# The first norm of a hybrid decoder block, rebuilt with two projections side by side and every engine in program order

## The chip, the cores and the metric

The kernel runs on one core of one Trainium2 chip. The metric is the device time of one launch in microseconds (us); the median of several runs is compared. PE (with PEld, its weight loads) is TensorE, DVE is VectorE, ACT is ScalarE, POOL is GpSimd and SP is SyncE, which issues the loads spoken of here.

## The reference

One decoder block over 512 tokens of width 1024, in float32. Only its beginning matters here:

```python
def rms_norm(x, g):
    y = xf * lax.rsqrt(jnp.mean(xf * xf, axis=-1, keepdims=True) + RMS_EPS)
    return y * g

h = rms_norm(x, ln1_g)
p = h @ w_in                  # 20 column tiles of 128 in the kernel
y_rwkv = rwkv7_mixer(p[..., :RWKV_COLS], ...)      # 14 of them
y_attn = rms_norm(swa_sink_attention(p[..., RWKV_COLS:] + b_attn, sinks), attn_norm_g)
x = x + concat(y_rwkv, y_attn) @ w_out
x = x + peer_ffn(rms_norm(x, ln2_g), ...)          # product-key retrieval, 16384 experts
return rms_norm(x, lnf_g)
```

The mixer needs a decay from a small projection (column tile 0, the low-rank inputs), and for each pair of heads j the tiles r, k and v (2+3j, 2+3j+1, 2+3j+2). Tile 3 is the first k. Inside the mixer a triangular 64x64 matrix is inverted for each chunk of 64 tokens; this inverse uses small masks.

## The kernel before, in words

x arrives transposed, as eight pieces `xT[:, k, :]` of 128 features x 512 tokens (256 KB each). The weight of the norm goes onto each piece (`h`, line 269 of the profile's numbering), the factor 1/rms of each token does not: it is put on after the projection, as `rb`, so that projections can run before the norm's sum is known. Products run in a split form: each float32 operand becomes a high part, cast on ScalarE (`split`, L166), and a low part, a subtraction on VectorE (L167), and each product is three (L176 to L178): high with high, low with high, high with low. A weight tile of one projection is two halves of 256 KB (`load_w`, L243) in three buffers `w`, with four buffers each for high and low parts.

The norm (`rms`) squares each piece on ScalarE (`take`, L216 and L219) into one of three buffers `n1sq` and adds the squares up on an engine given by name, here VectorE (L220); the last addition is always VectorE's. `scale` sums over the partitions with one-column products (`n1ss`, L225) and takes the reciprocal root in some eleven small VectorE instructions (`rsqrt`, L198 to L206). `spread` broadcasts the result with products (`n1b`, L232), and ScalarE copies it to `rb` (L283).

Projection 0 is written out, with the order of TensorE's instructions as traced (`manual_schedule` with TensorE alone), followed by `scale` and `spread`. For all else in the front the framework's list scheduler chooses the order on each engine: by priority in order of tracing, filling idle time with what is ready. `lora` then takes projection 0 through `shifted` (times `rb`, L307; the token shift, L308 and L309), tanh into `lw`, a memset of `lw` on GpSimd (L326) and the decay products (L330). `prepare(0)` follows with projections 3, 2 and 4. PSUM has two buffers with the tag `proj`; one is given back when `shifted` has multiplied it by `rb`.

The masks of the inverse, `lmask` and `id32`, are made on GpSimd at the very beginning: 20 memsets (L142), 20 selections (L144), 20 further selections (L147) and four for `id32` (L134). Their first reader is the inverse in `products(0)` (L473).

Loads are issued by SyncE in this order: the vectors, pieces 0 and 1 of x, the two halves of weight tile 0, pieces 2 to 7, the sinks, then what the front needs next.

Behind the front come a second block with TensorE's order written out (the output projection and the second norm, from about 312 us) and two with all engines in program order (retrieval and the expert sums).

Of the kernel before, what the change touches and what calls it, by code (L numbers as in the profile page):

```python
# [7 lines left out]
F32 = mybir.dt.float32  # L8
F32R = mybir.dt.float32r
# [8 lines left out]
S = 512  # L18
# [57 lines left out]
def _emit(ctx, tc, A, out, dbg, stop):  # L76
# [18 lines left out]
    for k in range(2):  # L95
        SY.dma_start(xT[:, k, :], A["xT"][:, k, :])
    sink = consts.tile([128, 8], F32, name="sink")

    def vcol(c):
        return vec[:, c:c + 1]  # L100
# [27 lines left out]


    lmask = consts.tile([128, 5, 32], F32, name="lmask")  # L130
    id32 = consts.tile([128, 32], F32, name="id32")
    for q in range(4):
        rows = slice(32 * q, 32 * q + 32)
        GP.affine_select(out=id32[rows], in_=ones[rows, :32], pattern=[[1, 32]],  # L134
                         compare_op=OP.is_equal, fill=0.0, base=0, channel_multiplier=-1)
    for lv in range(5):
        b = 1 << lv
        n = 32 // (2 * b)
        for q in range(4):
            rows = slice(32 * q, 32 * q + 32)  # L140
            m = lmask[rows, lv, :].rearrange("p (n w) -> p n w", w=2 * b)
            GP.memset(lmask[rows, lv, :], 0.0)  # L142

            GP.affine_select(out=m[:, :, b:2 * b], in_=ones[rows, :n * b].rearrange("p (n w) -> p n w", w=b),  # L144
                             pattern=[[-2 * b, n], [0, b]], compare_op=OP.is_ge, fill=0.0,
                             base=0, channel_multiplier=1)
            GP.affine_select(out=m[:, :, b:2 * b], in_=m[:, :, b:2 * b],  # L147
                             pattern=[[2 * b, n], [0, b]], compare_op=OP.is_ge, fill=0.0,
                             base=b - 1, channel_multiplier=-1)
# [87 lines left out]

    def load_w(src, name="w"):
        his, los = [], []
        for hf in range(2):  # L240
            ks = slice(4 * hf, 4 * hf + 4)
            w = wst.tile([128, 4, 128], F32, name=name, tag="w", bufs=3)
            SY.dma_start(w, src[:, ks])  # L243
            whi = wst.tile([128, 4, 128], F32R, name=name + "h", tag="wh", bufs=4)
            wlo = wst.tile([128, 4, 128], F32R, name=name + "l", tag="wl", bufs=4)
            split(whi, wlo, w)
            his += [whi[:, k] for k in range(4)]
            los += [wlo[:, k] for k in range(4)]
        return his, los

    first = {}

    def proj(i, m=128):
        whi, wlo = first.pop(i) if i in first else load_w(A["w_in"][i])
        p = pt("proj", "pj")
        yield from mm3_(p[:m], whi, wlo, hhi, hlo, m=m)
        return p[:m]


    first[0] = load_w(A["w_in"][0])  # L260
    for k in range(2, KD):
        SY.dma_start(xT[:, k, :], A["xT"][:, k, :])
    SY.dma_start(sink, A["sink"])

    take, scale, spread = rms(xp, KD, D, "n1", V)
    hhi, hlo = hl("h")
    for k in range(KD):
        h = xp.tile([128, S], F32, name="h", tag="h", bufs=3)
        V.tensor_scalar(h, xT[:, k, :], vcol(C_LN1 + k), None, op0=OP.mult)
        split(hhi[:, k, :], hlo[:, k, :], h)  # L270
        take(k, xT[:, k, :])
    with tc.manual_schedule(engines={mybir.EngineType.PE}):
        p0 = proj(0)
        while True:
            try:
                next(p0)
            except StopIteration as e:
                p0 = e.value
                break
        scale()  # L280
        pb = spread()
# [39 lines left out]

    def lora():
        yield from shifted(0, la, prep, p=p0)
# [1164 lines left out]
```

## Time and profile before

| | |
|---|---|
| median of 3 runs | 1629.78 us (1628.6 to 1633.54) |
| the profiled execution | 1630.73 us, span 1629.0 us |
| TensorE busy | 1572.6 us, 97% |
| VectorE busy | 1286.1 us, 79% |
| GpSimd busy | 742.4 us, 46% |
| ScalarE busy | 652.5 us, 40% |
| granted TensorE clock, mean | 0.995 |

The profile is of one execution. Its own time and its span differ by what lies around the first and the last instruction. Ends of products are modelled, so two neighbours overlap in the rows; the pitch from start to start is what one of them costs.

### The profile page before, as it was taken

How to read it: one execution, taken by the hardware profiler on the slowest of the kernel's cores; microseconds unless marked ns; L12 is line 12 of the kernel's file. 1: busy time of each engine (PE TensorE's matmuls, PEld its weight loads, DVE VectorE, ACT ScalarE, POOL GpSimd, SP SyncE). 2: the span in 40 equal slices, each digit the busy share in tenths (PEclk: the TensorE clock that was granted, in tenths of full speed). 3: DMA queues.
4: the chain of work that ended last, by engine and by line, in shares of the span. 5: the costliest groups of instructions: out<-in, count | busy, mean ns of one | idle time of the engine just before them, and what ended most of it. 6: DMA issues, size and time to landing. Idle time of an engine off the chain costs nothing.

```text
span 1629.0 us, 30768 instructions
## 1 busy us (share of the span) xinstructions
PE 1572.6 (97%) x11869; PEld 1366.7 (84%) x11869; DVE 1286.1 (79%) x2497; ACT 652.5 (40%) x1092; POOL 742.4 (46%) x711
## 2 busy tenths in 40 slices
PE   7999999899999889999999999999999999999997
PEld 4777777797999888888988888888888888888886
DVE  6666567756899999999677788777878877887896
ACT  5333345544444344454433333333333333333334
POOL 5121123244676512222155555555655556556582
PEclk9999999999999999999999999999999999999999
DMA  4111110333232269999999888889998988989793
GB/s 143 53 42 42 59 48 2 129 124 103 79 104 91 98 214 336 348 323 354 320 345 351 304 309 320 322 299 316 331 308 301 333 312 303 321 303 339 236 311 136
DMA packets 180548, 371.18 MB, mean 228 GB/s; under 512 B 17840, under 2 KB 102320, under 8 KB 180144
## 3 DMA queue, kind: packets, MB, share of 16 engines
q1 hardware_dynamic: 137488, 226.71, 40.6%
q0 software_dynamic: 36864, 134.23, 22.9%
q10 hardware_dynamic: 6048, 8.26, 1.4%
q8 instruction: 93, 1.52, 0.4%
q14 instruction: 55, 0.45, 0.1%
HBM read 333.62 MB, written 35.52 MB: 227 GB/s over the span
## 4 chain that ended last, share of the span: by engine, by line
PE 50%; DVE 11%; DMA 3%; issue 1%; ACT 1%; POOL 1%; SPq 0%; DVEq 0%; ACTq 0%
PE acc L1359 10%; PE acc L1358 10%; PE acc L1357 10%; PE pA L178 7%; PE pA L176 7%; PE pA L177 7%; DVE O L1228 3%; DVE ul L167 2%; DVE scr L1182 2%; DVE P L1233 2%; DMA u<-in_uT_dram 2%; DMA row<-in_vB_dram,ix 1%; DMA v<-in_vB_dram 0%; PE pG L1255 0%; POOL row L1169 0%
## 5 line engine op out<-in xcount | busy, mean ns | idle before, releaser
L178 PE MATMUL pA<-h2hi,ul 128*128 128x384 f32 x1024 | 346.2, 338 | 9.9 <-DVE ul L167 5.6
L176 PE MATMUL pA<-h2hi,uh 128*128 128x384 f32 x1024 | 350.3, 342 | 1.5 <-ACT actd L969 1.5
L177 PE MATMUL pA<-h2lo,uh 128*128 128x384 f32 x1024 | 344.1, 336 | 0.0
L1169 POOL DMA_INDIRECT row<-in_u_dram,ix x128 | 175.2, 1369 | 285.7 <-DVE scr L1182 247.7
L1359 PE MATMUL acc<-vl,wh 128*128 128x512 f32 x768 | 300.3, 391 | 1.5 <-DVE vl L167 1.5
L1358 PE MATMUL acc<-vh,wl 128*128 128x512 f32 x768 | 300.0, 391 | 0.2 <-DVE wl L167 0.2
L1357 PE MATMUL acc<-vh,wh 128*128 128x512 f32 x768 | 298.9, 389 | 1.3 <-ACT vh L166 1.3
L1169 POOL DMA_INDIRECT row<-in_vB_dram,ix x128 | 196.1, 1532 | 141.1 <-DVE x L1180 115.7
L167 DVE TENSOR_TENSOR vl<-v,vh 128x1024 fp32r<-128x1024 f32 x128 | 213.9, 1672 | 35.2 <-ACT vh L166 34.4
L178 PEld LDWEIGHTS pA<-h2hi,ul 128*128 128x128 f32 x1024 | 192.8, 188 | 14.8 <-DVE ul L167 10.5
L176 PEld LDWEIGHTS pA<-h2hi,uh 128*128 128x128 f32 x1024 | 193.0, 188 | 4.7 <-ACT actd L969 1.6
L177 PEld LDWEIGHTS pA<-h2lo,uh 128*128 128x128 f32 x1024 | 193.2, 189 | 3.0
L1180 DVE SCALAR_TENSOR_TENSOR x<-row,ac,x 128x1024 f32<-128x1024 f32 x128 | 173.2, 1353 | 7.9 <-DMA row<-in_vB_dram,ix 6.0
L1359 PEld LDWEIGHTS acc<-vl,wh 128*128 128x128 f32 x768 | 144.1, 188 | 32.2 <-DVE vl L167 2.2
L1357 PEld LDWEIGHTS acc<-vh,wh 128*128 128x128 f32 x768 | 144.2, 188 | 30.0 <-ACT vh L166 1.6
L1358 PEld LDWEIGHTS acc<-vh,wl 128*128 128x128 f32 x768 | 144.1, 188 | 29.4 <-DVE wl L167 0.6
L1182 DVE SCALAR_TENSOR_TENSOR scr<-row,h2g 128x1024 f32<-128x1024 f32 x128 | 158.2, 1236 | 1.3
L166 ACT CAST uh<-u 128x1024 fp32r<-128x1024 f32 x128 | 133.9, 1046 | 62.2 <-PE pA L177 29.5
L167 DVE TENSOR_TENSOR ul<-u,uh 128x1024 fp32r<-128x1024 f32 x109 | 134.0, 1230 | 20.1 <-ACT uh L166 17.0
L166 ACT CAST vh<-v 128x1024 fp32r<-128x1024 f32 x128 | 134.0, 1048 | 0.3 <-DMA gts<-gates 0.3
L969 ACT ACTIVATE act<-pA 128x384 f32<-128x384 f32 x86 | 42.2, 491 | 131.6 <-PE pA L178 131.5
L1256 ACT ACTIVATE gst<-pG 128x512 f32<-128x512 f32 x96 | 55.8, 597 | 97.6 <-PE pG L1255 95.9
(725 smaller groups left out, 2621.0 us busy)
## 6 DMA issues: line engine op xcount, KB each, us to landing
u<-in_uT_dram SPq DMA_DIRECT2D x128, 512.0 KB, 6.4
v<-in_vB_dram SPq DMA_DIRECT2D x128, 512.0 KB, 5.9
gts<-gates SPq DMA_DIRECT2D x384, 64.0 KB, 4.5
gates<-gst SPq DMA_DIRECT2D x11, 2048.0 KB, 11.5
w<-in_w_in_dram SPq DMA_DIRECT2D x40, 256.0 KB, 2.8
wq<-in_wq_dram SPq DMA_DIRECT2D x16, 512.0 KB
acts<-actd ACTq DMA_DIRECT2D x42, 192.0 KB, 6.3
act<-acts SPq DMA_DIRECT2D x42, 192.0 KB, 7.5
```

What stands on the lines that cost most here:

```text
L166: (hi_eng or SC.copy)(dst_hi, src)
L167: (lo_eng or V).tensor_tensor(out=dst_lo, in0=src, in1=dst_hi.bitcast(F32), op=OP.subtract)
L176: mm(ps, whi[k][:, :m], ahi[:, k], start=k == 0, stop=False)
L177: mm(ps, whi[k][:, :m], alo[:, k], start=False, stop=False)
L178: mm(ps, wlo[k][:, :m], ahi[:, k], start=False, stop=k == KD - 1)
L1169: GP.indirect_dma_start(r_, None, A["vB"].rearrange("b p d -> (b p) d") if w_ else A["u"], bass.IndirectOffsetOnAxis(ap=ix[:, w_, jj:jj + ...
L1180: V.scalar_tensor_tensor(x2[:, 0, :], r_, ac[:, jj:jj + 1], x2[:, 0, :], op0=OP.mult, op1=OP.add)
L1182: V.scalar_tensor_tensor(scr, r_, 1.0, h2g, op0=OP.mult, op1=OP.mult, accum_out=ac[:, jj:jj + 1])
L1256: SC.activation(gst[:, :, :, t4 * 4:t4 * 4 + 4].rearrange("p n g t -> p (n g) t"), p.rearrange("p t e -> p e t"), AF.Copy, scale=1.0 / GS)
L1357: mm(o, wh[:, ts], vh[:, ds_], start=b == 0, stop=False)
L1358: mm(o, wl[:, ts], vh[:, ds_], start=False, stop=False)
L1359: mm(o, wh[:, ts], vl[:, ds_], start=False, stop=b == 127)
```

## The change

The masks move from the beginning into `lora`, traced behind the first `shifted` and ahead of `lw`. The loads of x and of the weight tiles 0 and 3 are interleaved in one list. The loop over that list is traced with all five engines in program order, and the norm's additions go to GpSimd, but for the last. The products of projection 3 are traced beside those of projection 0, three pieces behind, and all of them ahead of the norm's sums. `prepare(0)` takes projection 3 as given. `load_w` is cut into `load_half` and `split_half`, which do together what it did.

```diff
-    for k in range(2):
-        SY.dma_start(xT[:, k, :], A["xT"][:, k, :])
...
-    lmask = consts.tile([128, 5, 32], F32, name="lmask")
-    id32 = consts.tile([128, 32], F32, name="id32")
-    for q in range(4):
...
+    def load_half(src, hf, name="w"):
+        w = wst.tile([128, 4, 128], F32, name=name, tag="w", bufs=3)
+        SY.dma_start(w, src[:, 4 * hf:4 * hf + 4])
+        return w
+
+    def split_half(w, name="w"):
+        whi = wst.tile([128, 4, 128], F32R, name=name + "h", tag="wh", bufs=4)
+        wlo = wst.tile([128, 4, 128], F32R, name=name + "l", tag="wl", bufs=4)
+        split(whi, wlo, w)
+        return [whi[:, k] for k in range(4)], [wlo[:, k] for k in range(4)]
...
-    first[0] = load_w(A["w_in"][0])
-    for k in range(2, KD):
-        SY.dma_start(xT[:, k, :], A["xT"][:, k, :])
+    ns = ExitStack()
+    ns.enter_context(tc.manual_schedule(engines={mybir.EngineType.Pool, mybir.EngineType.DVE, mybir.EngineType.Activation,
+                                                 mybir.EngineType.PE, mybir.EngineType.SP}))
+    wt = {}
+    arrive = (0, (0, 0), 1, (0, 1), 2, (3, 0), 3, 4, 5, (3, 1), 6, 7)
+    for a in arrive:
+        if isinstance(a, int):
+            SY.dma_start(xT[:, a, :], A["xT"][:, a, :])
+        else:
+            wt[a] = load_half(A["w_in"][a[0]], a[1])
     SY.dma_start(sink, A["sink"])
 
-    take, scale, spread = rms(xp, KD, D, "n1", V)
+    take, scale, spread = rms(xp, KD, D, "n1", GP)
     hhi, hlo = hl("h")
-    for k in range(KD):
-        h = xp.tile([128, S], F32, name="h", tag="h", bufs=3)
-        V.tensor_scalar(h, xT[:, k, :], vcol(C_LN1 + k), None, op0=OP.mult)
-        split(hhi[:, k, :], hlo[:, k, :], h)
-        take(k, xT[:, k, :])
-    with tc.manual_schedule(engines={mybir.EngineType.PE}):
-        p0 = proj(0)
...
+    early = {0: ([], []), 3: ([], [])}
+    for a in arrive:
+        if isinstance(a, int):
+            h = xp.tile([128, S], F32, name="h", tag="h", bufs=3)
+            V.tensor_scalar(h, xT[:, a, :], vcol(C_LN1 + a), None, op0=OP.mult)
+            split(hhi[:, a, :], hlo[:, a, :], h)
+            take(a, xT[:, a, :])
+        else:
+            for x, y in zip(early[a[0]], split_half(wt.pop(a))):
+                x += y
+    p03 = {i: pt("proj", "pj") for i in (0, 3)}
+    two = {i: mm3_(p03[i], *early[i], hhi, hlo) for i in (0, 3)}
+    for n in range(KD + 3):
+        next(two[0], None)
+        if n >= 3:
+            next(two[3], None)
+    scale()
+    pb = spread()
+    ns.close()
...
     def lora():
-        yield from shifted(0, la, prep, p=p0)
+        yield from shifted(0, la, prep, p=p03[0])
+
+
+        for q in range(4):
+            rows = slice(32 * q, 32 * q + 32)
+            GP.affine_select(out=id32[rows], in_=ones[rows, :32], pattern=[[1, 32]],
+                             compare_op=OP.is_equal, fill=0.0, base=0, channel_multiplier=-1)
+        for lv in range(5):
...
     def prepare(j):
         k = prep.tile([128, S], F32, name="k", tag="k", bufs=2)
-        yield from shifted(2 + 3 * j + 1, k, prep)
+        yield from shifted(2 + 3 * j + 1, k, prep, p=p03[3] if j == 0 else None)
```

## Rows read from the trace of the kernel before

**Rows 1.** The page's first part: busy time of each engine, its share of the span, and instructions.

```profile
PE 1572.6 (97%) x11869; PEld 1366.7 (84%) x11869; DVE 1286.1 (79%) x2497; ACT 652.5 (40%) x1092; POOL 742.4 (46%) x711
```

**Rows 2.** Busy time by stage. Columns: the stretch in us from the span's start, its length, then busy us (and instructions) of PE, PEld, DVE, ACT and POOL, the granted TensorE clock, the DMA engines' busy share and GB/s.

```profile
28.40:60.00 31.60, 31.60 (x190) 21.84 (x189) 22.82 (x53) 13.12 (x22) 3.46 (x11) 1.00 0.17 56
60.00:300.00 240.00, 235.20 (x4406) 177.07 (x4406) 157.34 (x416) 107.02 (x256) 57.16 (x96) 1.00 0.12 38
300.00:340.00 40.00, 35.07 (x288) 32.75 (x285) 26.03 (x70) 20.23 (x40) 11.38 (x8) 0.96 0.58 211
```

**Rows 3.** TensorE's products in order of time, 0 to 60 us. Columns here and in the other timelines: start us, us, engine, line, operation, out<-in, shapes, count, and in brackets the idle time before and what ended it.

```profile
10.55 0.63 PE L178 MATMUL pj<-hhi,wl 128*128 128x512 f32 x1
10.97 0.63 PE L176 MATMUL pj<-hhi,wh 128*128 128x512 f32 x1
...
17.14 0.67 PE L176 MATMUL pj<-hhi,wh 128*128 128x512 f32 x2
...
21.54 0.95 PE L225 MATMUL n1ss<-ones,n1acc 128*128 128x1 f32 x8
...
22.66 0.40 PE L176 MATMUL pj<-hhi,wh 128*128 128x512 f32 x1
...
24.06 0.39 PE L176 MATMUL pj<-hhi,wh 128*128 128x512 f32 x1
...
28.22 0.39 PE L178 MATMUL pj<-hhi,wl 128*128 128x512 f32 x1
28.45 0.40 PE L176 MATMUL pj<-hhi,wh 128*128 128x512 f32 x1
```

**Rows 4.** VectorE in order of time, 0 to 34 us.

```profile
7.80 1.49 DVE L167 TENSOR_TENSOR wl<-w,wh 128x512 fp32r<-128x512 f32 x2 [2.16 <-ACT wh L166]
...
14.44 0.47 DVE L269 TENSOR_SCALAR h<-xT,vec 128x512 f32<-128x512 f32 x1
...
15.43 0.47 DVE L269 TENSOR_SCALAR h<-xT,vec 128x512 f32<-128x512 f32 x1
15.83 0.68 DVE L167 TENSOR_TENSOR hlo<-h,hhi 128x512 fp32r<-128x512 f32 x1
16.43 0.68 DVE L220 TENSOR_TENSOR n1acc<-n1acc,n1sq 128x512 f32<-128x512 f32 x1
...
20.23 0.68 DVE L167 TENSOR_TENSOR hlo<-h,hhi 128x512 fp32r<-128x512 f32 x1
...
22.52 0.16 DVE L198 TENSOR_SCALAR rsq<-n1ss 128x4 f32<-128x4 f32 x1 [0.41 <-PE n1ss L225]
22.60 0.68 DVE L167 TENSOR_TENSOR wl<-w,wh 128x512 fp32r<-128x512 f32 x1
23.20 0.17 DVE L201 TENSOR_SCALAR rsq<-rsq 128x4 int32<-128x4 int32 x1
...
25.19 0.20 DVE L206 SCALAR_TENSOR_TENSOR n1rs<-rsq 128x4 f32<-128x4 f32 x1
...
27.40 0.69 DVE L307 TENSOR_TENSOR pr<-pj,rb 128x512 f32<-128x512 f32 x1 [0.69 <-ACT rb L283]
```

**Rows 5.** ScalarE in order of time, 0 to 34 us.

```profile
4.12 0.63 ACT L216 ACTIVATE n1acc<-xT 128x512 f32<-128x512 f32 x1 [2.04 <-DMA xT<-in_xT_dram]
7.15 0.62 ACT L166 CAST wh<-w 128x512 fp32r<-128x512 f32 x1 [2.40 <-DMA w<-in_w_in_dram]
...
14.94 0.62 ACT L166 CAST hhi<-h 128x512 fp32r<-128x512 f32 x1 [0.32 <-DVE h L269]
15.59 0.63 ACT L219 ACTIVATE n1sq<-xT 128x512 f32<-128x512 f32 x1
16.13 0.60 ACT L166 CAST hhi<-h 128x512 fp32r<-128x512 f32 x1
```

**Rows 6.** GpSimd's groups by line, 0 to 60 us (line, operation, out<-in, shapes, count | busy us, mean ns | idle before), and, as the last two rows, from its timeline the first selections for a mask and the first instruction on GpSimd that reads one.

```profile
L144 POOL TENSOR_SCALAR_AFFINE_SELECT lmask<-ones 32x16 f32<-32x16 f32 x20 | 8.6, 430 | 1.2
L147 POOL TENSOR_SCALAR_AFFINE_SELECT lmask<-lmask 32x16 f32<-32x16 f32 x20 | 6.3, 316 | 1.2
L142 POOL MEMSET lmask<- 32x32 f32 x20 | 2.8, 140 | 0.9
...
3.49 1.19 POOL L134 TENSOR_SCALAR_AFFINE_SELECT id<-ones 32x32 f32<-32x32 f32 x4
...
60.13 0.74 POOL L473 TENSOR_TENSOR Lb<-LC,lmask 128x256 f32<-128x256 f32 x1
```

**Rows 7.** GpSimd in order of time, 322 to 332 us: its nearest instructions with two tiles as inputs, the first three beside a busy VectorE.

```profile
323.51 3.22 POOL L853 TENSOR_TENSOR n2acc<-n2acc,n2sq 128x256 f32<-128x256 f32 x3 [27.84 <-ACT n2sq L852]
...
330.02 0.76 POOL L853 TENSOR_TENSOR n2acc<-n2acc,n2sq 128x256 f32<-128x256 f32 x1
330.72 2.41 POOL L167 TENSOR_TENSOR wql<-wq,wqh 128x1024 fp32r<-128x1024 f32 x1
```

**Rows 8.** Busy time and granted clock around the kernel's longest early stop of TensorE (columns as in rows 2).

```profile
318.00:322.00 4.00, 0.99 (x9) 0.79 (x7) 0.78 (x2) 0.00 (x0) 0.00 (x0) 1.00 0.95 394
322.00:324.00 2.00, 1.20 (x5) 1.23 (x6) 1.41 (x4) 1.32 (x4) 0.49 (x1) 0.58 1.02 418
324.00:326.00 2.00, 2.00 (x12) 2.00 (x12) 1.27 (x1) 1.96 (x3) 1.82 (x3) 0.57 0.79 322
```

**Rows 9.** The same view for a stretch of the first norm; the last two columns are the DMA engines.

```profile
14.00:22.00 8.00, 6.52 (x24) 3.75 (x23) 8.00 (x15) 5.08 (x9) 6.94 (x19) 1.00 0.04 14
```

More of the change, by code (lines that the diff above doesn't have):

```diff
@@ L127, in _emit @@
     V.tensor_copy(bones[:, 64:128], hind[:, 1:2].to_broadcast([128, 64]))
-    lmask = consts.tile([128, 5, 32], F32, name="lmask")
-    id32 = consts.tile([128, 32], F32, name="id32")
-    for q in range(4):
[L133 to L149, printed above, removed]
     c_ = consts.tile([128, 64], F32, name="c_")
@@ L240, in load_w @@
         for hf in range(2):
[L241 to L248, printed above, removed]
+            h_, l_ = split_half(load_half(src, hf, name), name)
+            his += h_
+            los += l_
         return his, los
-    first = {}
     def proj(i, m=128):
-        whi, wlo = first.pop(i) if i in first else load_w(A["w_in"][i])
+        whi, wlo = load_w(A["w_in"][i])
         p = pt("proj", "pj")
@@ L257, in proj @@
         return p[:m]
-    first[0] = load_w(A["w_in"][0])
-    for k in range(2, KD):
-        SY.dma_start(xT[:, k, :], A["xT"][:, k, :])
+    ns = ExitStack()
[8 more added lines that the diff above has]
+            wt[a] = load_half(A["w_in"][a[0]], a[1])
     SY.dma_start(sink, A["sink"])
-    take, scale, spread = rms(xp, KD, D, "n1", V)
+    take, scale, spread = rms(xp, KD, D, "n1", GP)
     hhi, hlo = hl("h")
-    for k in range(KD):
-        h = xp.tile([128, S], F32, name="h", tag="h", bufs=3)
-        V.tensor_scalar(h, xT[:, k, :], vcol(C_LN1 + k), None, op0=OP.mult)
-        split(hhi[:, k, :], hlo[:, k, :], h)
-        take(k, xT[:, k, :])
-    with tc.manual_schedule(engines={mybir.EngineType.PE}):
-        p0 = proj(0)
[L274 to L281, printed above, removed]
+    early = {0: ([], []), 3: ([], [])}
[17 more added lines that the diff above has]
+    ns.close()
     rb = prep.tile([128, S], F32, name="rb", tag="rb")
@@ L320, in _emit @@
     ld = [prep.tile([128, S], F32, name=f"ld{t}", tag=f"ld{t}") for t in range(NT)]
+    lmask = consts.tile([128, 5, 32], F32, name="lmask")
+    id32 = consts.tile([128, 32], F32, name="id32")
     def lora():
-        yield from shifted(0, la, prep, p=p0)
+        yield from shifted(0, la, prep, p=p03[0])
[4 more added lines that the diff above has]
+        for lv in range(5):
+            b = 1 << lv
+            n = 32 // (2 * b)
+            for q in range(4):
+                rows = slice(32 * q, 32 * q + 32)
+                m = lmask[rows, lv, :].rearrange("p (n w) -> p n w", w=2 * b)
+                GP.memset(lmask[rows, lv, :], 0.0)
+                GP.affine_select(out=m[:, :, b:2 * b], in_=ones[rows, :n * b].rearrange("p (n w) -> p n w", w=b),
+                                 pattern=[[-2 * b, n], [0, b]], compare_op=OP.is_ge, fill=0.0,
+                                 base=0, channel_multiplier=1)
+                GP.affine_select(out=m[:, :, b:2 * b], in_=m[:, :, b:2 * b],
+                                 pattern=[[2 * b, n], [0, b]], compare_op=OP.is_ge, fill=0.0,
+                                 base=b - 1, channel_multiplier=-1)
         lw = prep.tile([128, S], F32, name="lw", tag="t2")
```

## Prediction

> **What bounds the kernel now.** I read the page first, then the busy time by stage, then the order of each engine over the first 31 us. Over the whole span TensorE is busy 97% [rows 1]. By stage the last place with room is the front: from 28.4 us to 300 us TensorE is idle only 4.8 of 271.6 us (31.60 of 31.60 and 235.20 of 240.00 busy), and in the hand-over around 320 us 4.9 of 40 [rows 2]. So a delay or gain that TensorE takes before 28.4 us is passed on: there is no slack behind it that could swallow it, and little idle time that a new order there could win. What is to be read is therefore one number: when TensorE may start its third projection, the one traced for `r`.
>
> In the kernel before this is at 28.45 us [rows 3]. There are two PSUM buffers with the tag `proj`. Projection 0 and projection 3 hold both, and the third needs the one that the multiply by `rb` gives back. That multiply starts at 27.40 and ends at 28.09 [rows 4]. Projection 3's last product starts just ahead of 28.45, so here the chain of the norm and TensorE's work end together: while VectorE computes the reciprocal root (22.52 to 25.39), TensorE is fed by projection 3 [rows 3, 4]. That cover is what the change spends.
>
> **The chain behind the sums.** From the first sum product (21.54) to the end of the multiply (28.09) it is 6.55 us, of which 0.60 is a weight split that lies inside (22.60 to 23.20) [rows 3, 4]. Alone the chain takes 5.95 us. So the third projection starts at (start of the sums) + 5.95, and the break-even is a start of the sums at 28.45 - 5.95 = 22.5 us.
>
> **The change: the loop in program order.** For one piece of x the order is now: VectorE h, ScalarE hi, VectorE lo, ScalarE square. Each step waits for the one before it. From h to hi 0.50 (14.44 to 14.94), hi 0.62, hand-over 0.03 (7.15 + 0.62 to 7.80), lo until VectorE may start the next 0.60 (15.83 to 16.43): 1.75 us for each piece [rows 4, 5]. The next h stands behind this lo, so nothing overlaps the hi cast on VectorE. Where a half of a weight follows, ScalarE's cast stands behind the square: hi starts at 0.50, is followed by the square about 0.52 later, the cast 0.54 after that (15.59 to 16.13, the same pitch) at 1.56; it ends at 2.18, and the low part runs from 2.21, with VectorE free at 2.81 [rows 4, 5]. Four pieces are followed by a half, four are not: 4 x 2.81 + 4 x 1.75 = 18.24 us.
>
> The start is x's first landing at 4.12, which keeps its place in the queue. The second piece of x is now third in that queue, and the third entry landed at 7.15 in the kernel before, 0.22 later than the order would ask for it (4.12 + 2.81 = 6.93) [rows 5]. Later landings don't bind: all twelve pieces and two more transfers were in by about 14.3 us, since from 14 to 22 us the queues moved only 14 GB/s [rows 9]. The one wait that the change adds on SyncE is the fourth half, which needs the first of three buffers back (first low part done near 6.9). Queued behind it are only x's last two pieces, needed after 18 us, so I cost it at nothing; without that cover each us of it would cost one.
>
> So the last low part starts at 4.12 + 0.22 + 18.24 - 0.60 = 21.98 and ends at 22.66, against a start at 20.23 before [rows 4]. The six additions that leave VectorE give back nothing, because in this order VectorE is no longer full but waiting.
>
> **The change: two projections.** Projection 3 runs three pieces behind projection 0. When the last low part lands, what is left in TensorE's order is two products of projection 0 and the last four pieces of projection 3, twelve products: 14 x 0.233 (six products from 22.66 to 24.06) = 3.26 us [rows 3]. The sums stand behind them: 22.66 + 3.26 = 25.92. Then 5.95: the third projection starts at 31.87, against 28.45. That is +3.4 us, with TensorE idle through the reciprocal root, where projection 3 used to run.
>
> **The additions on GpSimd.** No row shows a 128x512 addition there. The nearest: 128x256 took 0.76 and 128x1024 took 2.41, in between 1.31; three of 128x256 beside a busy VectorE took 3.22, 1.07 each, 1.41 times as much [rows 7]. I take 1.5 us, nearer the clean value, since VectorE now idles between its two-input subtractions; bounds 1.31 and 1.31 x 1.41 = 1.85. All lie under the pitch of 1.75 to 2.81 or close to it, so the additions keep up. The sixth square ends about 20.9, its addition 22.4, the last addition (VectorE, behind the last low part) ends 23.3: hidden under TensorE's 25.92.
>
> **The masks.** The three groups of them take 8.6 + 6.3 + 2.8 = 17.7 us on GpSimd in sixty instructions [rows 6]. Their first user, at 60.13, is far off. But traced later is not run later: in the kernel before, a matmul pair of projection 3 runs at 17.14 amid a block whose TensorE order is written out for projection 0 [rows 3]. So I expect the scheduler to drop masks into GpSimd's gaps ahead of and between the additions. They began at 3.49 [rows 6]. About half ahead of the first addition would be 9 us from 3.5: GpSimd is free for it near 12 instead of at 8.8, where its square ends (7.15 + 1.02 + 0.63). Six additions of 1.5 and some fifteen more masks of 0.295 then end near 12 + 9 + 4.4 = 25.4, with 0.7 for the last addition 26.1, just behind 25.92. Bounds: nothing if few are dropped in, and 3.5 + 17.7 + 9.0 + 0.7 = 30.9, that is +5.0, if all are. Masks left over stand in front of the memset of `lw`, which gates the decay products; it is wanted near 34, and even with every mask ahead GpSimd is through by then. The Trainium skill (GPSIMD Engine Reference, 1. Specifications and 4.1 Engine selection) speaks against this part: it gives additions of two tiles to VectorE, GpSimd being about twice as slow at them, and lists VectorE instructions with two SBUF inputs among what GpSimd contends with. The trace agrees in sign, 1.07 against 0.76 [rows 7]; by that rule the additions sit at 1.85, the count above becomes 12 + 11.1 + 4.4 + 0.7 = 28.2, and the change costs +2.3 here where the row's middle gives +0.2. I take +0.2 for all of it, and +0.4 for weight splits of the third projection that slip into the chain as one did at 22.60.
>
> **Sum.** 3.4 + 0.2 + 0.4 = +4.0 us. The profiled execution took 1630.73 (span 1629.0), 0.95 above the median of the three runs, 1629.78. From 1630.73 the sum gives 1634.7, so about 1633.8 for a median. A measurement of this kernel tells about 0.3%, 4.9 us, from no change: the forecast is a small loss inside that.
>
> **Rivals.**
>
> *The engines overlap after all* (faster, inside 0.3%). If VectorE makes the next h while ScalarE casts, it is bound by its own work: 8 x (0.40 + 0.60) + 4 x 0.60 = 10.4 us with the pitches of [rows 4], some 11 with the last addition. The last low part ends near 15.5, the sums start at 18.8, the third projection at 24.7: -3.7, about 1626. It decides from a last low part before 28.45 - 5.95 - 3.26 = 19.2 us. For it: VectorE did run h ahead of lo in the kernel before. Against: there a scheduler chose the order, here the trace order is kept, and that has lo first. Chance 0.14.
>
> *GpSimd becomes the bound* (slower). Masks ahead of the additions, or additions at 1.85 and more beside VectorE. Three buffers hold the squares, so an addition that is late also holds ScalarE at the fourth square, and the hi casts behind it. It decides from a sixth addition that ends after 25.2; each us beyond costs one. Price up to +5.0 on the other +3.8: at its middle 1636.1, at its end 1638.6. For it: GpSimd was 17.7 us busy with masks. Against: they get shorter where VectorE is idle. Chance 0.20.
>
> *TensorE's clock falls* (slower). Between 318 and 322 us TensorE ran out of work, and from 322 to 326 its granted clock was 0.58 and 0.57 of 2.4 GHz, near the 1.2 GHz level [rows 8]. In the changed front it idles 2 to 3 us behind the sums and 1.4 before the third projection, with some 2 us of small products between. Four us at half rate cost 2 us. Or the products stay at the slow pitch seen at first (10.55 to 10.97, 0.42) up to the last piece: 14 x 0.19 = 2.7. Price +2 to +2.7: 1636. Against: two shorter gaps instead of one of 3.5. Chance 0.13.
>
> *The rest of the front falls out otherwise* (either sign): from `lora` on the order is the scheduler's, and it starts from another state. Bounds from [rows 2]: 4.8 us of idle time can be won, so at most -4.8 on +3.4; losses alike. Chance 0.08, half of it on each side.
>
> **Numbers.** The forecast itself has 0.45, of which a tenth spills over +4.9; overlap 0.14, of which 0.04 with a favourable order behind it passes -4.9; GpSimd 0.20 and clock 0.13, four fifths of both beyond +4.9; other 0.08, of which 0.04 passes -4.9 and 0.03 passes +4.9. Faster by over 0.3%: 0.04 + 0.04 = 0.08. Slower by over 0.3%: 0.045 + 0.265 + 0.03 = 0.34. Within: 0.58. The range runs from the overlap case, 1626, to the end of the GpSimd case with some clock, 1639; the likeliest case alone has 1631.5 to 1636.
>
> **What the profile of after would show.** Right: h, hi, lo, square in steps of about 1.75 and 2.81; the last low part near 22.7; the products of both projections done, and sums starting, near 26; TensorE idle through the reciprocal root; the third projection from about 32; then the old spacing. Wrong: h ahead of the previous lo; sums before 22.5; sums released by GpSimd's sixth addition or VectorE's last one (the second rival); products at double pitch at 23 or at 32 us (the third).

## The result: 19 us slower, and the profile after

The changed kernel took 1651.12 us (median of 5 runs, 1649.5 to 1651.56) against 1632.11 us for the kernel before in the same comparison (5 runs, 1628.6 to 1635.42): a ratio of 1.0119, 95% interval 1.0103 to 1.0134, or 19.0 us more. The forecast had +4.0. The single profiled execution of before, 1630.73 us, lies near the fast end of its runs; the changes of time below are taken between medians, the places from the traces.

TensorE works as many instructions as in [rows 1]. It is busy 1584.2 us in place of 1572.6, since a part of its products ran at the lower clock; the other 9 us of the longer span are idle time. The page of the changed kernel:

```profile
PE 1584.2 (96%) x11869; PEld 1375.3 (83%) x11869; DVE 1286.8 (78%) x2491; ACT 652.7 (40%) x1092; POOL 746.2 (45%) x717
```

TensorE of the changed kernel in order of time, 16 to 52 us. These rows answer to [rows 3]: the last products before the stop, the first behind it, the sums, the spread, the third projection and the decay products.

```profile
18.65 0.40 PE L154 MATMUL pj<-hhi,wl 128*128 128x512 f32 x1
24.26 0.80 PE L152 MATMUL pj<-hhi,wh 128*128 128x512 f32 x1 [5.22 <-ACT hhi L142]
...
38.34 0.95 PE L201 MATMUL n1ss<-ones,n1acc 128*128 128x1 f32 x8
42.29 2.05 PE L208 MATMUL n1b<-ident,n1rs 128*128 128x128 f32 x8 [3.00 <-DVE n1rs L182]
45.74 0.79 PE L152 MATMUL pj<-hhi,wh 128*128 128x512 f32 x1 [1.40 <-DVE pr L299]
...
50.07 2.40 PE L345 MATMUL pld<-wup,lw 128*128 128x512 f32 x5
```

The third projection starts at 45.74, where it stood at 28.45; the decay products start at 50.07, where they stood at 31.07. That is +17.3 and +19.0, and +19.0 is also the whole loss. The front holds all of it, as the prediction said a delay there would be passed on. The sums, forecast at 25.92, come at 38.34, 12.4 us late. GpSimd of the changed kernel, 20 to 40 us:

```profile
21.50 0.20 POOL L333 TENSOR_SCALAR_AFFINE_SELECT lmask<-ones 32x16 f32<-32x16 f32 x1
21.78 1.26 POOL L196 TENSOR_TENSOR n1acc<-n1acc,n1sq 128x512 f32<-128x512 f32 x1
23.11 0.68 POOL L336 TENSOR_SCALAR_AFFINE_SELECT lmask<-lmask 32x16 f32<-32x16 f32 x3
23.87 6.04 POOL L196 TENSOR_TENSOR n1acc<-n1acc,n1sq 128x512 f32<-128x512 f32 x4
30.12 1.47 POOL L196 TENSOR_TENSOR n1acc<-n1acc,n1sq 128x512 f32<-128x512 f32 x1 [0.20 <-ACT n1sq L195]
```

The first addition starts at 21.78, not near 12. Ahead of it GpSimd ran masks from 3.52 on without a gap to speak of, 61 of the 64 instructions that the diff had moved *behind* the norm in tracing order. An addition that late holds ScalarE, which waits at the fourth square for one of the three buffers. ScalarE of the changed kernel, 10 to 36 us:

```profile
14.92 0.62 ACT L142 CAST hhi<-h 128x512 fp32r<-128x512 f32 x1 [0.62 <-DVE h L259]
23.07 0.63 ACT L195 ACTIVATE n1sq<-xT 128x512 f32<-128x512 f32 x1 [7.54 <-POOL n1acc L196]
23.61 0.60 ACT L142 CAST hhi<-h 128x512 fp32r<-128x512 f32 x1
```

ScalarE stands for 7.54 us, and the cast of the next high part stands behind the square. VectorE stands as long, in the first of its rows below. Then comes what I had not priced (VectorE of the changed kernel, 22 to 35 us):

```profile
24.24 1.45 DVE L143 TENSOR_TENSOR hlo<-h,hhi 128x512 fp32r<-128x512 f32 x1 [7.58 <-ACT hhi L142]
26.34 1.03 DVE L143 TENSOR_TENSOR wl<-w,wh 128x512 fp32r<-128x512 f32 x1 [0.66 <-ACT wh L142]
27.30 1.50 DVE L259 TENSOR_SCALAR h<-xT,vec 128x512 f32<-128x512 f32 x1
28.72 1.75 DVE L143 TENSOR_TENSOR wl<-w,wh 128x512 fp32r<-128x512 f32 x1
30.39 1.74 DVE L143 TENSOR_TENSOR hlo<-h,hhi 128x512 fp32r<-128x512 f32 x1
32.06 0.47 DVE L259 TENSOR_SCALAR h<-xT,vec 128x512 f32<-128x512 f32 x1
33.22 0.69 DVE L143 TENSOR_TENSOR hlo<-h,hhi 128x512 fp32r<-128x512 f32 x1 [0.68 <-ACT hhi L142]
```

Beside an addition on GpSimd (23.87 to 31.59) a subtraction that takes 0.69 lasts 1.03 to 1.75 us, and `h`, which takes 0.47, lasts 1.50. From 32.06 on, with GpSimd idle, both have their old durations [rows 4].

Busy time by stage of the changed kernel (columns as in [rows 2]; the third number from the end is the granted clock):

```profile
18.00:24.20 6.20, 1.04 (x4) 0.46 (x3) 0.00 (x0) 1.13 (x2) 5.02 (x22) 0.79 0.00 0
24.20:28.00 3.80, 3.06 (x6) 1.78 (x6) 3.10 (x3) 1.67 (x4) 3.64 (x3) 0.50 0.00 0
28.00:35.00 7.00, 3.85 (x9) 2.52 (x9) 5.87 (x7) 2.92 (x5) 3.30 (x3) 0.50 0.22 75
35.00:38.40 3.40, 3.40 (x17) 2.75 (x15) 1.33 (x2) 0.67 (x2) 0.00 (x0) 0.96 0.34 98
38.40:42.20 3.80, 0.89 (x9) 0.80 (x7) 2.47 (x13) 0.57 (x1) 2.43 (x8) 0.99 0.35 114
42.20:45.70 3.50, 2.05 (x8) 1.78 (x8) 0.69 (x1) 0.59 (x1) 0.00 (x0) 0.50 0.02 6
45.70:49.00 3.30, 3.26 (x8) 2.59 (x9) 1.62 (x3) 2.08 (x3) 0.62 (x2) 0.51 0.00 0
```

Behind each stop of TensorE (5.22 us before 24.26, 3.00 before 42.29) the clock is at 0.50, the 1.2 GHz level, and stays there for some 10 and 7 us. In the kernel before, TensorE had no such stop around the sums, and from 21.5 to 28.4 us its clock was at 1.00.

### The profile page after: what moved, and what is told of

Read it like the earlier page. It is cut to its first block, busy times and chain, and to the rows that moved or that the text cites. A ratio compares the mean times of both kernels' runs of the same rounds, so it can differ in the third digit from the quotient of the medians.

```text
span 1649.4 us, 30772 instructions
## 1 busy us (share of the span) xinstructions
PE 1584.2 (96%) x11869; PEld 1375.3 (83%) x11869; DVE 1286.8 (78%) x2491; ACT 652.7 (40%) x1092; POOL 746.2 (45%) x717
## 4 chain that ended last, share of the span: by engine, by line
PE 51%; DVE 10%; DMA 2%; issue 1%; POOL 1%; ACT 1%; SPq 1%; DVEq 0%; ACTq 0%
PE acc L1374 10%; PE acc L1373 10%; PE acc L1372 10%; PE pA L154 7%; PE pA L152 7%; PE pA L153 7%; DVE O L1243 3%; DVE scr L1197 2%; DVE ul L143 2%; DVE P L1248 2%; PE pG L1270 1%; DMA row<-in_vB_dram,ix 0%; SPq L1311 0%; DMA u<-in_uT_dram 0%; DMA gates<-gst 0%
```

## The experiments

Two theories stood at first. Q: GpSimd is late, because the masks stand ahead of the additions, and the three buffers turn that into a hold of the other engines. R: the written order and the lost cover cost that much by themselves, with the clock. The runs led to a third part that neither had. The kernels, with the start of the third projection and of the decay products in their traces:

| kernel | ratio to before (95%) | third projection | decay products |
|---|---|---|---|
| before | 1 | 28.45 | 31.07 |
| after | 1.0119 (1.0103 to 1.0134) | 45.74 | 50.07 |
| a, masks behind | 1.0095 (1.0078 to 1.0112) | 41.20 | 46.49 |
| b, seven buffers | 1.0095 (1.0077 to 1.0113) | 42.03 | 46.91 |
| c, additions on VectorE | 1.0051 (1.0034 to 1.0068) | 35.60 | 40.12 |
| d, masks moved alone | 0.9996 (0.9984 to 1.0009) | 29.05 | 31.62 |
| e, sums ahead | 1.0026 (1.0017 to 1.0035) | 32.42 | 35.31 |
| f, no tile h | 0.9987 (0.9978 to 0.9997) | 26.43 | 29.31 |
| g, TensorE fed | 1.0031 (1.0019 to 1.0043) | 34.80 | 37.69 |
| h, two projections alone | 1.0031 (1.0019 to 1.0043) | 34.85 | 39.09 |
| i, additions on GpSimd alone | 1.0066 (1.0048 to 1.0084) | 39.17 | 41.73 |
| j, table early | 0.9994 (0.9985 to 1.0003) | 25.71 | 29.17 |
| k, idle additions | one run, 1657.02 us | 42.17 | 46.36 |
| l, idle copies | one run, 1649.55 us | 38.24 | 43.53 |

### a: the masks kept behind the additions

The masks of the changed kernel are made from a tile that is computed from `lw`, so no scheduler can run them early:

```diff
+        ones2 = consts.tile([128, 32], F32, name="ones2")
+        GP.tensor_scalar(ones2, lw[:, 0:32], 0.0, 1.0, op0=OP.mult, op1=OP.add)
+        GP.memset(lmask.rearrange("p l w -> p (l w)"), 0.0)
...
-            GP.affine_select(out=id32[rows], in_=ones[rows, :32], pattern=[[1, 32]],
+            GP.affine_select(out=id32[rows], in_=ones2[rows, :32], pattern=[[1, 32]],
```

> The changed kernel, with the masks made from a tile that exists only once lw does (and one memset of lmask in place of twenty), so that none of them can run ahead of an addition. Theory Q, the additions stood behind the masks on GpSimd and the full square buffers then held ScalarE: the first addition starts by 9 us instead of 21.78, no hold at the fourth square, the third projection starts at 32 to 37 us instead of 45.74 (32 if the additions leave VectorE alone, 37 if each of six costs VectorE 0.8 us), and the whole comes to between 0 and 10 us above the kernel before. Rival R, the written-out order itself (waiting in turn, lost cover) is the loss: third projection within 3 us of 45.74, the whole still 15 us or more above the kernel before.

The additions were on time, each behind its square (GpSimd of this kernel):

```profile
8.81 1.27 POOL L196 TENSOR_TENSOR n1acc<-n1acc,n1sq 128x512 f32<-128x512 f32 x1 [5.54 <-ACT n1sq L195]
...
15.91 1.27 POOL L196 TENSOR_TENSOR n1acc<-n1acc,n1sq 128x512 f32<-128x512 f32 x1 [2.27 <-ACT n1sq L195]
```

No hold was left, and still the last low part ended at 28.19 and the third projection started at 41.20; the whole was 15.5 us above before (0.0095 of 1632), a miss for both theories as written. VectorE of this kernel tells why:

```profile
9.39 1.25 DVE L143 TENSOR_TENSOR wl<-w,wh 128x512 fp32r<-128x512 f32 x1 [0.47 <-ACT wh L142]
...
15.88 1.58 DVE L259 TENSOR_SCALAR h<-xT,vec 128x512 f32<-128x512 f32 x1
```

Each of the six additions stretches the one VectorE instruction beside it to 1.25 to 1.61 us, and in program order everything stands behind that. Taking the masks out of the way was worth 4.5 us at the third projection (45.74 to 41.20). All of it is lost again: the late masks, 44.4 to 58.4 us, stand ahead of a memset that the next tile waits for (VectorE of this kernel).

```profile
58.60 0.75 DVE L301 SCALAR_TENSOR_TENSOR r<-pr,vec,r 128x512 f32<-128x512 f32 x1 [2.93 <-POOL pr L298]
```

At the decay products kernel a was 3.6 us ahead of the changed kernel (46.49 to 50.07). At the first products of a later tile, `pg`, it was 0.9 us behind (72.87 to 72.00). The two profiled executions took 1651.54 and 1651.12 us. So the trace doesn't show where the 0.0024 between the two ratios comes from, and their intervals overlap.

### b: seven buffers for the squares

```diff
-tag="rsq", bufs=3)
+tag="rsq", bufs=7)
```

> The changed kernel with seven buffers for the squares instead of three; masks as in the changed kernel. Theory Q with the hold through the buffers: ScalarE no longer waits at the fourth square, the last low part ends near 23 us instead of 33.9, but the sixth addition still ends near 31, so the sums start near 31 to 32 instead of 38.34 and the whole gains 5 to 8 us on the changed kernel. If the buffers do not matter and late additions alone are the bound: sums within 1.5 us of 38.34, the whole within 3 us of the changed kernel.

The hold is gone and the low parts are done at 22.87. Now the wait is at the other end of the same queue (VectorE of this kernel):

```profile
22.18 0.69 DVE L143 TENSOR_TENSOR hlo<-h,hhi 128x512 fp32r<-128x512 f32 x1 [0.69 <-ACT hhi L142]
32.97 0.69 DVE L196 TENSOR_TENSOR n1acc<-n1acc,n1sq 128x512 f32<-128x512 f32 x1 [10.09 <-POOL n1acc L196]
```

Sums at 33.72, 1.7 later than the latest expected, and a gain of about 4 us (1.0119 to 1.0095, with intervals that overlap) for 5 to 8. The first addition itself came later, at 24.18 in place of 21.78: VectorE worked on, and the masks beside it took longer. The hold was only the place where GpSimd's lateness showed. This kernel also tests the prediction's first step: with no addition beside VectorE, the last low part ended at 22.87, forecast 22.66.

### c: the additions back on VectorE, all else as changed; d: the masks moved alone

```diff
-    take, scale, spread = rms(xp, KD, D, "n1", GP)
+    take, scale, spread = rms(xp, KD, D, "n1", V)
```

> The changed kernel with all seven additions on VectorE; GpSimd makes masks only. Theory Q: nothing waits for GpSimd; VectorE's steps grow by up to 0.6 us, the last low part ends near 25 us, sums near 28, the third projection at 34 to 36, the whole 4 to 10 us above the kernel before. Rival R: third projection within 3 us of 45.74. Against the kernel with masks behind: this one is the faster if additions on GpSimd slow VectorE by more than the 0.6 us that an addition takes there.

As expected: third projection 35.60, the whole 8.3 us above before (0.0051 of 1632). TensorE of c:

```profile
28.31 0.95 PE L201 MATMUL n1ss<-ones,n1acc 128*128 128x1 f32 x8
32.26 1.95 PE L208 MATMUL n1b<-ident,n1rs 128*128 128x128 f32 x8 [3.00 <-DVE n1rs L182]
35.60 0.79 PE L152 MATMUL pj<-hhi,wh 128*128 128x512 f32 x1 [1.40 <-DVE pr L299]
```

So the additions on GpSimd, masks and hold included, cost 0.0068, or 11 us of the 19. Kernel d is before with the block of masks traced in `lora`, as the diff has it, and nothing else:

> The kernel before with one part of the change alone: the masks traced inside lora. Theory Q: the scheduler drops them into GpSimd's idle time all the same, they run from about 3.5 us, nothing waits for them, and the time is that of the kernel before within 3 us. If the move itself (its place ahead of lw) costs: the memset of lw and with it the decay products come late, and the whole is 3 us or more slower.

No change, as expected. Moving a block later in tracing order did not move it on the chip: the selections start at 3.52, where they stood at 3.49.

### h: two projections ahead of the sums, in the kernel before

```diff
-        p0 = proj(0)
+        for i in (0, 3):
+            p0 = proj(i)
...
-        yield from shifted(2 + 3 * j + 1, k, prep)
+        yield from shifted(2 + 3 * j + 1, k, prep, p=p03[3] if j == 0 else None)
```

> The kernel before with one part alone: the products of projections 0 and 3 both ahead of the sums in TensorE's written order; masks, additions and all other orders as before. Theory (lost cover): 21 products of 0.233 now stand ahead of the sums, so the sums start near 26.5 instead of 21.54 and the third projection at 32.5 to 33.5 instead of 28.45, with up to 3 us more for the clock: the whole 4 to 8 us above the kernel before. If TensorE's idle time can be filled otherwise: less than 3 us.

5.1 us slower (0.0031), inside 4 to 8. The third projection, at 34.85, is 1.35 us behind the 32.5 to 33.5 expected, which left up to 3 us more for the clock. TensorE of h:

```profile
27.45 0.95 PE L225 MATMUL n1ss<-ones,n1acc 128*128 128x1 f32 x8
31.40 2.05 PE L232 MATMUL n1b<-ident,n1rs 128*128 128x128 f32 x8 [3.00 <-DVE n1rs L206]
34.85 0.80 PE L176 MATMUL pj<-hhi,wh 128*128 128x512 f32 x1 [1.40 <-DVE pr L310]
```

The same 3.00 and 1.40 us of idle TensorE as in c and after, and the same slow spread (2.05 for what took 0.94 before). The loss of cover needs neither the written order of the other engines nor additions on GpSimd.

### e and g: the cover given back, or the clock held up

Kernel e is c with the sums ahead of the trailing nine products of projection 3; g is c with 12 products that nobody reads behind the sums and 6 behind the spread:

```diff
-    for n in range(KD + 3):
+    for n in range(KD):
...
     scale()
+    for _ in two[3]:
+        pass
     pb = spread()
```

> The kernel with all additions on VectorE, and the norm's sums ahead of the products of projection 3 that are then left (12 of them less the three that run beside the last addition), which so lie under the reciprocal root. Theory: what is left of the loss, 8 us in the kernel with additions on VectorE, is lost cover and, with it, TensorE's clock. Then the sums start at 25.5 to 26 instead of 28.31, the granted clock stays up, the third projection starts at 31.5 to 32.5 instead of 35.60 and its products take 0.23 us each from the first; the whole is 5 to 7 us below the kernel with additions on VectorE, 1 to 3 above the kernel before. Rival: only the order counts and not the clock; third projection near 33, whole 2 to 3 us below.

```diff
     scale()
+    feed(12)
     pb = spread()
+    feed(6)
```

> The kernel with all additions on VectorE, with 12 more products of no use between the sums and the spread, and 6 behind the spread; nothing else moves. It measures the clock alone: the sums stay at 28.3. If the fall of the clock costs time, the spread's products take 1.05 us instead of 1.95, the third projection starts near 34.7 instead of 35.60 at 0.23 us a product instead of 0.43, and the whole is 2 to 3.5 us shorter than with additions on VectorE alone. If it does not, within 1 us or longer.

In e the sums stood at 26.28, 0.3 behind the range expected, and the third projection at 32.42, inside it; the whole gained 4.1 us on c, less than the 5 to 7 expected, and was 4.2 above before in place of 1 to 3. The busy time by stage (columns as in [rows 2]) shows the clock over one stretch, first in c:

```profile
32.20:35.60 3.40, 1.95 (x8) 1.68 (x8) 0.69 (x1) 0.60 (x2) 0.00 (x0) 0.52 0.03 10
```

and in g:

```profile
32.20:35.60 3.40, 3.33 (x18) 2.62 (x19) 0.76 (x2) 1.41 (x3) 0.00 (x0) 1.00 0.05 18
```

With the same sums at 28.31, the decay products came 2.43 us sooner in g (40.12 to 37.69) and the whole 3.3 us (1.0051 to 1.0031). So the clock behind one 3 us stop costs 2.4 us up to the decay products, read from one execution of each kernel; useless work in the gap bought it back. The 3.3 us by the ratios are no firmer than that, since each of the two is uncertain by 2 to 3 us.

### i: the additions on GpSimd, in the kernel before

```diff
-    take, scale, spread = rms(xp, KD, D, "n1", V)
+    take, scale, spread = rms(xp, KD, D, "n1", GP)
```

> The kernel before with one edit: the squares of the first norm are summed on GpSimd; masks, projections and the order of the engines stay as they were. Theory X (an addition on GpSimd makes the VectorE instruction beside it last 1.2 to 1.7 us in any order of the work): the low parts, which ended near 20 us in before, end 3 to 7 us later, the sums come 4 to 9 us later, and the third projection, at 28.45 in before, stands at 33 to 39; the whole 4 to 10 us longer. Theory Y (the additions hurt only because the masks stand ahead of them and the buffers of the squares run out): here the masks stand ahead of them too, so a hold of ScalarE of several us must be seen, and the VectorE instructions outside that hold keep 0.48 and 0.69.

10.8 us slower (0.0066), above the range of theory X, with the third projection at 39.17 for 33 to 39. Both theories hold in part. The hold is there, in ScalarE's order of kernel i:

```profile
21.05 0.63 ACT L219 ACTIVATE n1sq<-xT 128x512 f32<-128x512 f32 x1 [7.90 <-POOL n1acc L220]
```

and in VectorE's order of i:

```profile
26.87 4.07 DVE L167 TENSOR_TENSOR hlo<-h,hhi 128x512 fp32r<-128x512 f32 x3 [11.62 <-ACT hhi L166]
```

Of the three low parts there, one keeps 0.69 us and two, beside additions, take 1.77 and 1.76. How the 10.8 us divide between the hold and the stretched instructions, this run doesn't show. The one-word change costs 10.8 us in the old order and 11.1 in the new one (c to after), the same within their intervals.

### k and l: GpSimd work that nobody waits for

Both are c with the masks behind, as in a, and for pieces 1 to 6 one GpSimd instruction into a tile that is never read: in k an addition, in l a copy.

```diff
+                GP.tensor_tensor(out=junk, in0=xT[:, a, :], in1=hhi[:, a, :].bitcast(F32), op=OP.add)
```

> The kernel c_adds_on_vector (all sums on VectorE) with the masks put behind the decay's activation and six additions of two inputs on GpSimd (input and high part of a piece into a tile that nobody reads), so nothing waits for GpSimd ahead of the sums. Theory X (the addition itself stops VectorE): each VectorE instruction beside one lasts 1.2 to 1.7 us in place of 0.48 or 0.69, the last low part ends 4 to 8 us later than 24.89 in c_adds_on_vector, the third projection at 38 to 44 (35.60 there). Theory Z (VectorE was late in the other kernels because of what waited for GpSimd's result): the last low part within 1 us of 24.89. The late masks cost some 4 us behind the third projection, so only what lies ahead of it is compared.

```diff
-                GP.tensor_tensor(out=junk, in0=xT[:, a, :], in1=hhi[:, a, :].bitcast(F32), op=OP.add)
+                GP.tensor_copy(junk, hhi[:, a, :].bitcast(F32))
```

> k_idle_additions with a copy (one input) of the high part in the place of each addition of two inputs. If it is the second input that stops VectorE: its instructions beside the copies keep 0.48 and 0.69, last low part within 1.5 us of 24.89. If any GpSimd instruction that streams a 128x512 tile does: 1.0 to 1.7 us as beside the additions, and the last low part 3 us late or more.

VectorE of k, the low part ahead of the first addition, the first addition with a neighbour, and the last without:

```profile
8.07 0.69 DVE L143 TENSOR_TENSOR hlo<-h,hhi 128x512 fp32r<-128x512 f32 x1 [0.48 <-ACT hhi L142]
8.68 1.76 DVE L196 TENSOR_TENSOR n1acc<-n1acc,n1sq 128x512 f32<-128x512 f32 x1
...
31.22 0.68 DVE L196 TENSOR_TENSOR n1acc<-n1acc,n1sq 128x512 f32<-128x512 f32 x1
```

The neighbour of the first, on GpSimd of k:

```profile
8.12 1.77 POOL L264 TENSOR_TENSOR junk<-xT,hhi 128x512 f32<-128x512 f32 x1 [4.87 <-ACT hhi L142]
```

Each VectorE addition beside one on GpSimd lasts 1.76 or 1.77 us; the last one, with GpSimd idle, 0.68. The GpSimd addition is longer too, 1.77 for 1.27 in a. The last low part ends at 31.30, 6.4 us behind c, and the third projection stands at 42.17, as theory X had it. Nothing waits for these additions, so it is not the wait for a result. The three rows read as turns: the low part that started first, at 8.07, keeps its 0.69; the GpSimd addition that started behind it, at 8.12, is the one that is 0.5 us longer; and VectorE's addition, started at 8.68, ends at 10.44, 0.55 us behind the end of GpSimd's (9.89). In l the VectorE additions beside the copies last 1.10 us (VectorE of l, then GpSimd):

```profile
8.75 1.10 DVE L196 TENSOR_TENSOR n1acc<-n1acc,n1sq 128x512 f32<-128x512 f32 x1
...
8.17 1.13 POOL L264 COPY junk<-hhi 128x512 f32<-128x512 f32 x1 [4.91 <-ACT hhi L142]
```

and the last low part ends at 27.38, 2.5 us behind c: between the two answers expected. One input disturbs VectorE too, with +0.42 in place of +1.08. Here, too, VectorE's addition ends 0.55 us behind its neighbour (9.85 and 9.30). So the copy may cost less only because it is shorter; no run separates its length from the number of its inputs.

### f and j: a front that is not slower

Kernel f is e without the tile `h`: ScalarE makes the high part straight from x, VectorE the low part in one instruction. That takes one of three steps out of each piece.

```diff
-            V.tensor_scalar(h, xT[:, a, :], vcol(C_LN1 + a), None, op0=OP.mult)
-            split(hhi[:, a, :], hlo[:, a, :], h)
+            SC.activation(hhi[:, a, :], xT[:, a, :], AF.Identity, scale=vcol(C_LN1 + a))
+            V.scalar_tensor_tensor(hlo[:, a, :], xT[:, a, :], vcol(C_LN1 + a), hhi[:, a, :].bitcast(F32),
+                                   op0=OP.mult, op1=OP.subtract)
```

> The kernel with the sums ahead and additions on VectorE, and no h tile: ScalarE casts the high part from x times the norm's weight directly, VectorE makes the low part in one instruction (x times weight minus high part), so no engine waits in turn. Theory: the ping-pong of VectorE and ScalarE set the pace of 1.75 and 2.81 us. Then eight low parts of 0.67, four weight parts and seven additions of 0.60 on VectorE, 12 us, end near 17.5 to 18.5, the sums start by 19, the third projection at 24 to 25.5, the whole 2 to 5 us below the kernel before. If arrival of x or TensorE's early slow products set the pace: third projection at 27 or later, the whole within 2 us of the kernel before.

The sums moved to 19.79 and the third projection to 26.43, 2.0 us ahead of before, though 0.9 behind the expected range. The whole is 0.9987 of before (0.9978 to 0.9997): the only kernel of the study whose interval lies below 1, by 2 us, which is inside the 0.3% that the prediction took for no change. Its table load stood at 4.25 to 5.53 us, behind the wait for the first piece of x. Kernel j adds a tiny activation ahead of all:

```diff
+    SC.activation(warm, ones[:, 0:1], AF.Identity, scale=ones[:, 0:1])
```

> The kernel f_no_h_tile (written order without the tile h, additions on VectorE, sums ahead of the trailing products) with one tiny activation ahead, so that ScalarE loads its table while the first transfer is still under way. If the load, which lay at 4.25 to 5.53 in f_no_h_tile, was on the chain: first high part near 4.3 to 4.5 instead of 5.54, third projection at 25.0 to 25.6 (26.43 there, 28.45 in before), the whole 2 to 4.5 us below before. If it was hidden by a later transfer of the input: third projection within 0.4 of 26.43 and the whole as there (0.9987 of before).

The first high part came at 4.13 in place of 5.54, the third projection at 25.71 (0.1 outside the range), 0.7 ahead of f. The whole didn't follow: 0.9994 (0.9985 to 1.0003), where 2 to 4.5 us were expected. The gain had been spent by the decay products, 29.17 against 29.31 in f. GpSimd of j shows on what:

```profile
25.67 2.71 POOL L522 MEMSET TF<- 32x256 f32 x8
28.44 0.10 POOL L303 MEMSET pr<- 128x1 f32 x1
28.60 0.52 POOL L346 MEMSET lw<- 32x512 f32 x1
```

The memset of `lw` stands behind the eight memsets of `TF`, though ScalarE had written its part of that tile by 27.87. In f, at 28.70, it had waited 0.35 us for ScalarE. So behind f GpSimd is the next bound of the front. An order with that memset first wasn't run.

## Why the prediction was wrong, step by step

**What bounds the kernel: right.** The decay products are 19.0 us late and the whole is 19.0 us longer. In the kernels b to g, i and j, too, the two agree to within 1.6 us; in h they don't (8.0 and 5.1; its profiled execution, 1640.07 us, was 2.4 above its median). That they agree in a (15.4 and 15.5) is luck, since the late masks cost it over 4 us behind the decay products; k and l, with the same late masks, have one run each.

**The pitch of the written order: right.** The pieces followed each other by 2.81 and 1.75 us up to the hold, and in b, without a hold, the last low part ended at 22.87 for 22.66. So close a hit has some luck in it: the 0.22 us of waiting for the second piece of x did not come (its `h` follows the first by 2.82 in b), and the first piece was 0.27 later than the 4.12 assumed. That VectorE would idle and not overlap (against the first rival) was right too.

**Fourteen products behind the last low part: right in number, wrong in price.** 3.26 us were forecast. c, at full clock, took 3.42 (24.89 to 28.31), after, at half clock for a part, 4.43 (33.91 to 38.34).

**The chain of 5.95 us: right at full clock only.** e took 6.14 from the sums to the third projection; c 7.29, h and after 7.40. Of the 1.15 us between e and c, 0.81 lies behind the start of the spread, which is slow in c; 0.34 lies ahead of it, where a weight split slipped in (VectorE of c, 29.57), as the +0.4 of the prediction allowed.

**The additions on GpSimd: the step that failed.** They were priced, together with the masks, at +0.2 us; the runs show 11 (after less c, and i). The working says "I take 1.5 us, nearer the clean value ... so the additions keep up", and "The six additions that leave VectorE give back nothing". Their own duration was close: 1.26 to 1.61 us in after. What was missing is the other direction: each makes the VectorE instruction beside it last 0.6 to 1.1 us longer (in a). I had weighed only GpSimd's slow-down, from the 1.41 of [rows 7], though I had noted there that VectorE was busy beside those three, and had not read how long its instructions took. The price was in the trace of before, beside the last row of [rows 7], where GpSimd's subtraction starts at 330.72 and takes 2.41 (VectorE of before, that neighbour and the same form with GpSimd idle):

```profile
330.81 3.40 DVE L167 TENSOR_TENSOR wol<-wo,woh 128x1024 fp32r<-128x1024 f32 x1 [0.30 <-ACT woh L166]
...
376.43 1.23 DVE L167 TENSOR_TENSOR ul<-u,uh 128x1024 fp32r<-128x1024 f32 x1 [2.34 <-ACT uh L166]
```

[rows 7] calls only its first three beside a busy VectorE; this one was, too. The GpSimd duration was clean, as I took it (2.42 at 379.15, with VectorE idle); it was VectorE that paid, 3.40 for 1.23. The Trainium skill (GPSIMD Engine Reference, 8. Key points) names contention with VectorE instructions of two SBUF inputs. The traces agree (0.68 to 1.76 in k), and they add that a one-input instruction, `h`, goes from 0.48 to 1.58 (in a). The Trainium skill (Advanced Engine Details and Errata, Mode Summary) says that GpSimd's and VectorE's two-port instructions block each other, which speaks of both sides; whether `h` is one of those, no run here shows.

**The masks: the mechanism right, the share wrong.** I expected about half ahead of the first addition, and 61 of 64 ran there. The numbers that should have decided it were in [rows 6]: GpSimd was free from 3.5 us, the masks are 17.7 us of work, and 3.5 + 17.7 = 21.2 is close to the 21.78 at which the first addition started. The scheduler did not stop at the first square. The rival "GpSimd becomes the bound" was what happened, with the hold it named, yet its price stopped at +5.0, because it counted GpSimd's own work to its end and not what was left behind the hold: three more pieces on ScalarE and on a slowed VectorE, and the products behind the last of them.

**The clock: a rival that came on top.** "TensorE's clock falls" had been priced at +2 to +2.7. One such stop costs 2.4 us at the decay products (c against g); after has two. I had treated it as an alternative to a late GpSimd, while the one causes the other: the hold made a stop of 5.22 us.

**The sum, mended.** From 31.87, forecast, to 45.74, measured, it is 13.9 us: the last low part ended 11.25 later than forecast (33.91 for 22.66), of which 7.54 is the hold and the rest mostly the stretched instructions behind it; 1.2 for slow products; 1.45 for the slow chain. Then 1.7 more up to the decay products, 4.33 us behind the third projection in place of 2.62. By the ratios the loss, 0.0119, divides into 0.0031 for the lost cover with its clock (h), 0.0020 for the written order (c less h) and 0.0068 for the additions on GpSimd (after less c): 5.1, 3.3 and 11.1 us. From the intervals each is uncertain by some 2 to 4 us, so the middle part isn't told from nothing; i gives the last part as 10.8 by itself. By the places of the decay products, one execution each, the parts are 8.0, 1.0 and 10.0.

What stays open is how the 8 us that are not the additions divide between cover and order, and how the 11 divide: of the 11 us, a divides some 4.5 (masks ahead) from 5.6 (additions beside VectorE, c to a) at the third projection, but that is read from one execution of each kernel, and kernel a loses its lead again behind the decay products.

## What to carry to other kernels

Before work is given to an engine with time to spare, price what it does to its neighbour: look for rows where both run at once, and read the durations of both. Ask of every filler that a scheduler may place (masks, memsets) what keeps it behind the new work; tracing order did not, a data dependence did. And when rivals feed each other (late additions, a stopped TensorE, a lower clock), give the case in which they come together its own price.

## What the runs showed of the hardware that was not expected

- A 128x512 float32 addition takes 0.68 us on VectorE (k, the last one) and 1.26 on GpSimd with VectorE idle (after, the first one). Which of two neighbours gets longer went by the start: in k a VectorE subtraction that was ahead by 0.05 us kept its 0.69 and the GpSimd addition took 1.77, and the VectorE addition behind that took 1.76. Beside a GpSimd copy of one input VectorE's addition takes 1.10 (l). The small masks (32x16) left VectorE's 0.48 and 0.69 as they were and paid themselves: in after a selection took 0.74 at 15.60, beside a subtraction, and 0.19 at 19.92, with VectorE idle.
- Behind stops of TensorE of 3.00 us (c, h) the granted clock was 0.50 to 0.52 over the next 6.8 us in c, though there were products in that time; with products in the gap (g) it stayed at 1.00.
- ScalarE's table load stood at 0.79 us in before and in c, though the first instruction that used it waited until 4.12 (for a transfer) and 4.67 (for VectorE). In f it stood at 4.25, behind the wait for the first piece of x; there the first instruction reads two transferred tiles, x and the weight of the norm. Why it waited in f alone isn't shown; a tiny instruction ahead of it brought it back to 0.79 (j).
